# Weight sums and operand sums of the prologue formed by adding transfers, and the output weights copied later, in a hybrid Mamba-2 and attention layer

## Chip, cores and metric

The kernel runs on one core of one Trainium2 chip. The metric is the device time of one execution in microseconds (us), the median of several runs. Before the change it is 1277.86 us (three runs, 1277.46 to 1280.73).

## What is computed

One decoder layer on 1024 tokens of width 1024, all in float32. The change touches only the first product and the way its operands are made:

```python
h    = RMSNorm_pre(x)                                  # x, h: 1024 x 1024
proj = jnp.einsum('bld,de->ble', h, w_in)              # w_in: 1024 x 9248
z_ssm, xbc, dt_raw, q, k, v, f_raw, z_att, g_ssm, g_att = jnp.split(proj, ...)
...
merge = sigmoid(g_ssm) * (A @ w_branch_ssm) + sigmoid(g_att) * (B @ w_branch_att)
out   = merge @ w_out;  x <- x + RMSNorm_post(out)
```

A is a chunked SSD scan and B is causal attention with a forgetting bias; both follow later and are left alone.

## The kernel before

**Products.** The projections are done by a Strassen-Winograd scheme: seven products in place of eight. The right operand is h transposed, cut into four blocks of 512 x 512: B11, B21 (first 512 tokens), B12, B22 (last 512). Its seven forms are kept in SBUF as tiles x0 to x6: x0 = B11, x1 = B21, x2 = -B22, x3 = T1 = B12 - B11, x4 = -T2 with T2 = B22 - T1, x5 = T3 = T2 - B11, x6 = T4 = T2 - B21. Each has a high part and a low part (x5h and x5l), so that three fast matmuls stand for one float32 matmul. The high part is a ScalarE copy that rounds, the low part a VectorE subtraction (`put`, L1211).

**Weights.** The left operand comes in pairs of 128-column units (class `Pair`, L320). A pair has four blocks a11, a12, a21, a22 of 128 x 512, loaded into `raw` tiles (L342, six buffers). Product 1 takes a11, product 2 a12, product 4 a22, product 5 the sum s1 = a21 + a22, product 6 s2 = s1 + a11, product 3 s2 + a12, product 7 a11 + a21. The sums are VectorE additions (L355, L371). `split` (L345) then makes the high part on ScalarE (L349) and the low part on VectorE (L350) of a `wop` tile, of which there are four.

**Order.** `Stream` (L461) holds the list of (pair, product) steps. For the first three pairs p, q, r it begins p1, q1, p2, q2, p6, p5, p7, p4, p3, q6, q5, q7, r1, q4, q3. Each step is twelve matmuls at L128, done in two halves. `ahead` (L597) prepares the step three places later when a step starts, and `load_more` (L509) issues the next loads when the blocks that they replace have been used. TensorE's order is that of the program; a scheduler orders the other engines' instructions at build time.

**The prologue** (L1167 to L1280) loads eight token tiles `xt`, normalises them (the first four on VectorE, L1201, the last four on GpSimd, L1203), and transposes them on TensorE into `pt` (L1209). For the first 512 tokens ScalarE or VectorE scales the transposes into `low` (L1228, L1230), which holds B11 and B21. For the last 512 it goes through four columns j = 0 to 3. In each one, ScalarE scales two transposes into `up` (B12) and `b22` (both L1248), four float32 matmuls with 32 columns of weights go into `df` (L1251), VectorE forms t1 and t2, and half a product step follows. Then VectorE turns `low` into T3 and T4 in place (L1262, L1263). The tile t2 comes from a pool of four buffers named `th` that outputs use as well. After the columns come the parts of T3, T4 and -B22. `dft` (L1265) takes `df` out of PSUM.

**Queues.** All loads of weights and tokens are issued from SyncE's queue (SP), in order. Twelve copies of the output weights from the input to `wo_dram` (L1237, 256 KB each) stand there behind the first loads; they are read again near the end of the kernel. GpSimd's queue (POOL) issues transfers too, the first of them at 656.7 us of the span; no transfer adds to its destination.

Of the kernel before, what the change touches and what calls it, by code (L numbers as in the profile page):

```python
# [16 lines left out]
P = 128  # L17
T = 1024
D = 1024
NK = D // P  # L20
KH = NK // 2
# [65 lines left out]
def hybrid_layer(ctx: ExitStack, tc, a, out):  # L87

    nc = tc.nc
# [43 lines left out]
    def pin(op):  # L133
        return tc.keep_in_program_order(op)
# [185 lines left out]
    class Pair:  # L320
# [3 lines left out]


        USES = {"a11": (1, 6, 7), "a12": (2, 6), "a21": (6, 7), "a22": (6, 4)}

        def __init__(self, keys, handlers, ops=None, adds=nc.vector):
            self.keys, self.handlers = keys, handlers
            self.ops = xop if ops is None else ops  # L330
            self.adds = adds
            self.raw, self.op, self.prepared = {}, {}, set()
            self.s1, self.sums = None, 0

        def load(self, names):
            for n in names:
                if self.keys[0][0] == "merged":
                    h, t = int(n[2]) - 1, self.keys[int(n[1]) - 1][1]
                    self.raw[n] = fin["merged"][:, h * KH : (h + 1) * KH, t * P : (t + 1) * P]
                    continue  # L340
                t = wp.tile([P, KH, P], F32, tag="raw", bufs=6, name="raw")
                pin(nc.sync.dma_start(t, column_halves(self.keys[int(n[1]) - 1])[int(n[2]) - 1]))  # L342
                self.raw[n] = t

        def split(self, which, src):  # L345
            op = wp.tile([P, 2, KH, P], F32R, tag="wop", bufs=4, name="wop")
# [11 lines left out]
        def prepare(self, which):  # L358
            r = self.raw
            self.prepared.add(which)  # L360
            if which in (5, 6) and self.s1 is None:
# [99 lines left out]
    class Stream:  # L461
# [6 lines left out]
        def __init__(self, pairs, double, last):  # L468
# [40 lines left out]
        def load_more(self):  # L509

            while self.loads:
                old = self.loaded[-6:-4]
                if self.loads[0][0].keys[0][0] == "merged":
                    old = []
                    if "merged" not in fin:
                        return
                if not all(set(p.USES[n]) <= p.prepared for p, n in old):
                    return
                self.load_next()

# [646 lines left out]
    with tc.tile_pool(name="pro", bufs=1, reuse_waits="tile", side="right") as pro, tc.tile_pool(  # L1167
# [3 lines left out]
        nc.scalar.dma_start(wdf, a["wdf"])  # L1171
        preg = pro.tile([P, NK], F32, name="preg")
        nc.scalar.dma_start(preg, a["cst"][:, 80:88])
        ss = pro.tile([P, NT], F32, name="ss")
        rstd = pro.tile([P, NT], F32, name="rstd")
        low = pro.tile([P, NK, HALF], F32, name="low")
# [14 lines left out]
        def norm_tiles(hf, tiles):  # L1191
            for t, xt in enumerate(tiles, 4 * hf):
                sqt = small("sqt").bitcast(BF16)
                if t in (1, 3):
                    nc.vector.tensor_tensor_reduce(sqt, xt, xt, 1.0, 0.0, ALU.mult, ALU.add, ss[:, t : t + 1])
                else:
                    nc.scalar.activation(sqt, xt, AF.Square, accum_out=ss[:, t : t + 1])
                nc.scalar.activation(rstd[:, t : t + 1], ss[:, t : t + 1], AF.Sqrt, bias=epst, scale=1.0 / D)
                nc.vector.reciprocal(rstd[:, t : t + 1], rstd[:, t : t + 1])
                if hf == 0:  # L1200
                    nc.vector.tensor_scalar(xt, xt, rstd[:, t : t + 1], None, ALU.mult)  # L1201
                else:
                    nc.gpsimd.tensor_scalar(xt, xt, rstd[:, t : t + 1], None, ALU.mult)  # L1203

        def turned(tiles, k):
            pt = prop.tile([P, HALF], F32, tag="pt", bufs=2, name="pt")
# [16 lines left out]
        tiles2 = load_tiles(1)  # L1223
        stream.begin()
        for k in range(NK):
            pt = turned(tiles, k)
            if k > 1:
                nc.scalar.activation(low[:, k, :], pt, AF.Copy, scale=preg[:, k : k + 1])  # L1228
            else:
                nc.vector.tensor_scalar(low[:, k, :], pt, preg[:, k : k + 1], None, ALU.mult)  # L1230
            put("b11" if k < KH else "b21", k % KH, low[:, k, :])
            if k >= KH:
                stream.halves(1)
        norm_tiles(1, tiles2)

        for k, h in [(k, h) for j in range(KH) for k, h in ((j, 0), (j + KH, 0), (j + KH, 1))]:
            pin(nc.sync.dma_start(wo_dram[k, :, half(h)], a["wo"][k * P : (k + 1) * P, half(h)]))  # L1237

        b22 = []
        for j in range(KH):  # L1240
# [20 lines left out]
            with tc.issue_after(last[1]) if j == KH - 1 else nullcontext():  # L1261
# [3 lines left out]
        nc.scalar.activation(dft, df, AF.Identity, bias=bdf)  # L1265
        stream.halves(1)

        with tc.issue_after(last[0]), tc.issue_after(last[1]):
# [524 lines left out]
```

## Time and profile before

| | us |
|---|---|
| median of three runs | 1277.86 |
| profiled execution, its time | 1273.87 |
| profiled execution, its span | 1272.2 |
| TensorE busy in the span | 1246.1 |
| VectorE, ScalarE, GpSimd busy | 1012.9, 794.3, 319.3 |
| VectorE busy from 46 to 61 us | 15.0 of 15 |

The profile is one execution. Its views are the page (totals), the waits (who waited for whom), the chain of waits (the work that ended last, followed back step by step), the timeline (instructions in order, with start, duration and the idle time just before), and a table of busy time by stretches. In a timeline row "x3" joins three instructions. An L number is a line of the kernel before.

### The profile page before, as it was taken

To read this page: it belongs to the slowest core of one execution; us is meant where nothing else is said; L and a number is where in the kernel's file an instruction comes from. 1 tells how busy PE (TensorE), PEld (TensorE's weight loads), DVE (VectorE), ACT (ScalarE), POOL (GpSimd) and SP (SyncE) were. 2 spreads that over 40 slices of the span, in tenths; PEclk is the share of its full clock that TensorE was granted. 3 is DMA by queue.
4 is the path that set the end of the run, shared out by engine and by line. 5 is a ranking of instruction groups with operands and counts; after the bars stand their busy time and mean duration, and the time that the engine had idled before them with its cause. 6 is when DMAs were issued, how large, how long until landed. Compare 5 with 4: busy or idle time off the path is not lost.

```text
span 1272.2 us, 20822 instructions
## 1 busy us (share of the span) xinstructions
PE 1246.1 (98%) x6926; PEld 982.3 (77%) x6926; DVE 1012.9 (80%) x1994; ACT 794.3 (62%) x1737; POOL 319.3 (25%) x322
## 2 busy tenths in 40 slices
PE   5999999999999999999999999999999999999997
PEld 3678888888888888888887777777777777778886
DVE  7988886988888978997767676767789767886975
ACT  7745665556665765566555666666687666844753
POOL 4000440013400241115102124223112212356062
PEclk9999999999999999999999999999999999999999
DMA  8232452545436533744447576666687657766933
GB/s 300 69 120 76 146 162 88 191 152 182 138 101 215 175 127 117 219 146 140 142 149 252 162 228 212 217 214 218 232 286 263 224 184 249 249 221 199 364 110 105
DMA packets 152236, 233.56 MB, mean 184 GB/s; under 512 B 15201, under 2 KB 60737, under 8 KB 152129
## 3 DMA queue, kind: packets, MB, share of 16 engines
q1 hardware_dynamic: 136064, 196.08, 47.7%
q10 hardware_dynamic: 10560, 18.06, 3.8%
q0 software_dynamic: 5504, 18.09, 3.7%
q8 instruction: 54, 0.88, 0.3%
q14 instruction: 54, 0.43, 0.1%
HBM read 162.99 MB, written 72.34 MB: 185 GB/s over the span
## 4 chain that ended last, share of the span: by engine, by line
PE 86%; DMA 4%; DVE 4%; ACT 4%; issue 1%; SPq 0%; POOL 0%; DVEq 0%; ACTq 0%; POOLq 0%
PE pb L128 36%; PE pc L128 21%; PE pd L128 7%; PE av L128 5%; PE pt L131 5%; PE s L128 5%; PE yps L128 2%; PE st L128 1%; ACT ex L1509 1%; DMA xt<-in_x 1%; PE tr L131 1%; PE tr_v L131 1%; DMA v<-v_dram 1%; PE df L128 1%; DVE wop L350 1%
## 5 line engine op out<-in xcount | busy, mean ns | idle before, releaser
L350 DVE TENSOR_TENSOR wop<-sum,wop 128x512 fp32r<-128x512 f32 x180 | 140.2, 780 | 53.6 <-ACT wop L349 52.6
L349 ACT ACTIVATE wop<-sum 128x512 fp32r<-128x512 f32 x180 | 112.5, 626 | 109.0 <-DVE sum L355 52.4
L1509 ACT ACTIVATE ex<-ex,nm 128x512 f32<-128x512 f32 (+1 forms) x192 | 116.2, 606 | 71.9 <-DVE nm L1505 71.6
L402 ACT ACTIVATE s<-pb 128x512 f32<-128x512 f32 x144 | 85.3, 593 | 98.2 <-PE pb L128 96.2
L128 PE MATMUL pb<-x0h,wop 128*128 128x512 f32 x384 | 131.5, 399 | 0.0
L128 PE MATMUL pb<-x6h,wop 128*128 128x512 f32 x384 | 129.5, 395 | 1.3 <-ACT s L402 1.3
L128 PE MATMUL pb<-x5h,wop 128*128 128x512 f32 x384 | 130.1, 396 | 0.7 <-ACT s L402 0.7
L350 DVE TENSOR_TENSOR wop<-raw,wop 128x512 fp32r<-128x512 f32 x144 | 105.4, 733 | 31.8 <-ACT wop L349 31.5
L128 PE MATMUL pc<-x3h,wop 128*128 128x512 f32 x384 | 129.8, 396 | 0.5 <-DVE ot L419 0.4
L128 PE MATMUL pc<-x2h,wop 128*128 128x512 f32 x384 | 130.2, 397 | 0.0
L128 PE MATMUL pb<-x4h,wop 128*128 128x512 f32 x384 | 129.1, 395 | 0.0
L1505 DVE CUSTOM_DVE_ANT_0 ex<-s,fb 128x512 f32<-128x512 f32 (+1 forms) x192 | 96.8, 552 | 20.0 <-PE s L128 14.8
L349 ACT ACTIVATE wop<-raw 128x512 fp32r<-128x512 f32 x144 | 89.7, 623 | 14.7 <-PE pd L128 6.1
L128 PE MATMUL pd<-x1h,wop 128*128 128x512 f32 x288 | 96.3, 394 | 0.0
L128 PEld LDWEIGHTS pb<-x6h,wop 128*128 128x128 f32 x384 | 72.1, 188 | 18.6 <-issue 2.0
L128 PEld LDWEIGHTS pb<-x5h,wop 128*128 128x128 f32 x384 | 72.1, 188 | 18.4 <-issue 2.0
L128 PEld LDWEIGHTS pb<-x0h,wop 128*128 128x128 f32 x384 | 72.6, 189 | 17.6 <-issue 2.9
L128 PEld LDWEIGHTS pc<-x3h,wop 128*128 128x128 f32 x384 | 72.1, 188 | 17.7 <-issue 1.5
L128 PEld LDWEIGHTS pc<-x2h,wop 128*128 128x128 f32 x384 | 72.1, 188 | 17.4 <-issue 2.4
L128 PEld LDWEIGHTS pb<-x4h,wop 128*128 128x128 f32 x384 | 72.1, 188 | 16.7 <-issue 1.9
L211 POOL TENSOR_TENSOR wd<-wd 128x256 f32<-128x256 f32 x32 | 32.4, 1011 | 205.0 <-DMA wd<-in_wo 135.0
L131 PE MATMUL pt<-ident,ex 128*128 128x128 f32 x576 | 75.1, 273 | 2.0 <-ACT ex L1509 1.4
(318 smaller groups left out, 2993.6 us busy)
## 6 DMA issues: line engine op xcount, KB each, us to landing
raw<-in_wu SPq DMA_DIRECT2D x128, 256.0 KB
csb<-cs_dram SPq DMA_DIRECT2D x32, 256.0 KB
q<-q_dram SPq DMA_DIRECT2D x32, 256.0 KB
k<-k_dram SPq DMA_DIRECT2D x16, 512.0 KB
fb<-f_dram SPq DMA_DIRECT2D x16, 512.0 KB
rb<-st_dram SPq DMA_DIRECT2D x48, 128.0 KB
wd<-in_wo SPq DMA_DIRECT2D x40, 128.0 KB
xt<-in_x SPq DMA_DIRECT2D x8, 512.0 KB
```

The source lines that it names most:

```text
L128: return tc.keep_in_program_order(nc.tensor.matmul(*args, **kw))
L131: return tc.keep_in_program_order(nc.tensor.transpose(out_, in_, idn))
L211: pin(nc.gpsimd.tensor_tensor(t[out_], t[a_], t[b_], ALU.subtract))
L349: nc.scalar.activation(op[:, 0], src, AF.Copy)
L350: nc.vector.tensor_tensor(op[:, 1], src, op[:, 0], ALU.subtract)
L402: nc.scalar.activation(s, ps, AF.Copy)
L1505: nc.vector.tensor_tensor_reduce(o, s[e][:, 0:w], fb[hp, h][:, e, 0:w], 1.0, 3.0e38, ALU.add, ALU.min, nm)
L1509: pin(nc.scalar.activation(o, o, AF.Exp, scale=-1.0, bias=nm, accum_out=hd.at(hd.sm, i, h, e)))
```

## The change

For the first three pairs, `gather` starts s1 (and for p also s2) as a load of a21 from DRAM (issued from SP, L360 of the changed kernel) to which GpSimd's queue adds a22 and a11 by transfers with `accum_op` (L354 there). The sum a11 + a21 is made by adding a11 to the loaded a21 in place, and a12 is added to s2 after product 6 has taken it. q and r still form s2 with VectorE. That is eleven adding transfers. `low` is stored with its sign turned, so that T3 and T4 become sums: `low += t2` is an adding transfer from SBUF to SBUF for all of T4 and three quarters of T3; the last of T3 stays on VectorE. `behind` holds the first adding transfers until GpSimd has normalised its last token tile. `FEWER` says which products still read a loaded block. `ahead` prepares nothing when step 1 starts and two steps when step 2 starts. The twelve copies to `wo_dram` are issued behind the prologue.

```diff
+        FEWER = {"a11": (1, 6), "a12": (2,), "a21": (7,), "a22": (4,)}
...
+            if self.gathers and self.s1 is not None and "a21" in names:
+                self.add(self.raw["a21"], "a11")
+        def add(self, t, n):
+            with tc.issue_after(self.behind) if self.behind else nullcontext():
+                nc.gpsimd.dma_start(t, self.source(n), accum_op=ALU.add)
+        def gather(self):
+            for n in range(2 if self.gathers == "fully" else 1):
+                t = wp.tile([P, KH, P], F32, tag="sum", bufs=2, name="sum")
+                nc.sync.dma_start(t, self.source("a21"))
+                self.add(t, "a22")
+                if n == 0:
+                    self.s1 = t
+                else:
+                    self.add(t, "a11")
+                    self.s2 = t
+            if "a21" in self.raw:
+                self.add(self.raw["a21"], "a11")
...
             elif which == 6:
-                self.s2 = self.total(self.s1, r["a11"])
+                if self.gathers != "fully":
+                    self.s2 = self.total(self.s1, r["a11"])
                 self.split(6, self.s2)
+                if self.gathers:
+                    self.add(self.s2, "a12")
+                    return
...
+            elif which == 7 and self.gathers:
+                self.split(7, r["a21"])
...
+            p.gathers, q.gathers, r.gathers = "fully", "partly", "partly"
...
+            following = self.pairs[self.pairs.index(p) + 1 :][:1]
+            if which == 5 and following and following[0].gathers:
+                following[0].gather()
...
-            if self.at + 3 < len(self.steps):
-                p, which = self.steps[self.at + 3]
+            for n in {1: (), 2: (4, 5)}.get(self.at, (self.at + 3,)):
...
+        less = pro.tile([P, NK], F32, name="less")
+        nc.vector.tensor_scalar(less, preg, -1.0, None, ALU.mult)
...
-                nc.scalar.activation(low[:, k, :], pt, AF.Copy, scale=preg[:, k : k + 1])
+                nc.scalar.activation(low[:, k, :], pt, AF.Copy, scale=less[:, k : k + 1])
...
-        for k, h in [(k, h) for j in range(KH) for k, h in ((j, 0), (j + KH, 0), (j + KH, 1))]:
-            pin(nc.sync.dma_start(wo_dram[k, :, half(h)], a["wo"][k * P : (k + 1) * P, half(h)]))
+        stream.pairs[0].behind = stream.pairs[1].behind = norm_tiles(1, tiles2)
+        stream.pairs[0].gather()
...
-                nc.vector.tensor_tensor(t1, up[0], b11, ALU.subtract)
+                nc.vector.tensor_tensor(t1, up[0], b11, ALU.add)
...
-                nc.vector.tensor_tensor(b11, t2, b11, ALU.subtract)
-                nc.vector.tensor_tensor(b21, t2, b21, ALU.subtract)
+            if j < KH - 1:
+                nc.gpsimd.dma_start(b11, t2, accum_op=ALU.add)
+            else:
+                nc.vector.tensor_tensor(b11, t2, b11, ALU.add)
+            nc.gpsimd.dma_start(b21, t2, accum_op=ALU.add)
...
             put("-b22", j, b22[j], -1.0, order=pin)
+        for k, h in [(k, h) for j in range(KH) for k, h in ((j, 0), (j + KH, 0), (j + KH, 1))]:
+            pin(nc.sync.dma_start(wo_dram[k, :, half(h)], a["wo"][k * P : (k + 1) * P, half(h)]))
```

TensorE's instructions stand in the same order before and after, from the first to the last. On the other engines the order differs in the prologue and shortly behind it.

**ScalarE in the third column.** The first `up` and `b_419` below belong to the third column, `th` at L629 is the tanh of the first output of q, and its table load stands ahead of it. Before:

```order
L1213 ACTIVATE x4h<-th 128x512
L349 ACTIVATE wop<-sum 128x512
L1248 ACTIVATE up<-pt,preg 128x512
L1248 ACTIVATE b_419<-pt,preg 128x512
L629 ACT_TABLE_LOAD
L629 ACTIVATE th<-th 128x512
L630 DMA gs_dram<-th 128x512
L1213 ACTIVATE x3h<-th 128x512
L1248 ACTIVATE up<-pt,preg 128x512
```

After, with the names as above (`b_425` is the same tile, the three `wop` rows are s2, s1 and a11 + a21 of p):

```order
L1290 ACTIVATE up<-pt,preg 128x512
L666 ACT_TABLE_LOAD
L666 ACTIVATE th<-th 128x512
L1290 ACTIVATE b_425<-pt,preg 128x512
L667 DMA gs_dram<-th 128x512
L1257 ACTIVATE x3h<-th 128x512
L374 ACTIVATE wop<-sum 128x512 x2
L374 ACTIVATE wop<-raw 128x512
L1257 ACTIVATE x4h<-th 128x512
L1290 ACTIVATE up<-pt,preg 128x512
```

The table load and the tanh now stand between the third column's two copies out of PSUM, and three weight splits stand in front of the fourth column's.

**GpSimd's queue** from the last token tiles on. Before:

```order
L1203 TENSOR_SCALAR xt_182<-xt_182,rstd_144 128x1024
L1203 TENSOR_SCALAR xt_184<-xt_184,rstd_144 128x1024
L1203 TENSOR_SCALAR xt_186<-xt_186,rstd_144 128x1024
L1203 TENSOR_SCALAR xt_188<-xt_188,rstd_144 128x1024
L1291 AFFINE_SELECT tri_627<-onesr_625 128x128
```

After (`sum_330` is s1 of p, `sum_333` its s2, `raw_196` and `raw_368` the blocks a21 of p and q; `th_360` and `th_409` are t2 of the first two columns):

```order
L1246 TENSOR_SCALAR xt_194<-xt_194,rstd_150 128x1024
L354 DMA sum_330<-in_wu 128x512
L354 DMA sum_333<-in_wu 128x512
L354 DMA raw_196<-in_wu 128x512
L354 DMA raw_368<-in_wu 128x512
L1304 DMA low_151<-th_360 128x512
L1307 DMA low_151<-th_360 128x512
L354 DMA sum_333<-in_wu 128x512
L1304 DMA low_151<-th_409 128x512
L1307 DMA low_151<-th_409 128x512
```

Six adding transfers now stand in one queue ahead of the one that completes s2 of p.

**VectorE behind the fourth column**, from the first output of q's product 2 (`th<-pd,s`) on. Before:

```order
L415 TENSOR_TENSOR th<-pd,s 128x512
L1215 TENSOR_TENSOR x3l<-th,x3h 128x512
L350 TENSOR_TENSOR wop<-raw,wop 128x512
L1217 SCALAR_TENSOR_TENSOR x4l<-th,x4h 128x512
L1262 TENSOR_TENSOR low<-th,low 128x512
L1263 TENSOR_TENSOR low<-th,low 128x512
L1215 TENSOR_TENSOR x5l<-low,x5h 128x512 x3
L661 SCALAR_TENSOR_TENSOR th<-th 128x512
L1215 TENSOR_TENSOR x5l<-low,x5h 128x512
L1215 TENSOR_TENSOR x6l<-low,x6h 128x512 x3
L350 TENSOR_TENSOR wop<-sum,wop 128x512
```

After:

```order
L446 TENSOR_TENSOR th<-pd,s 128x512
L1261 SCALAR_TENSOR_TENSOR x4l<-th,x4h 128x512
L375 TENSOR_TENSOR wop<-raw,wop 128x512
L1259 TENSOR_TENSOR x5l<-low,x5h 128x512 x4
L698 SCALAR_TENSOR_TENSOR th<-th 128x512
L1259 TENSOR_TENSOR x6l<-low,x6h 128x512 x3
L375 TENSOR_TENSOR wop<-sum,wop 128x512
```

The two sums and an x3l have left this stretch. In both kernels it goes on with four x2l, the last x6l, a sum (s2 of q), `th<-pc,s`, a memset and `summing`, the tile that TensorE needs for the transpose of `dft`; after the change two more weight splits stand ahead of the memset. From `th<-pd,s` up to the memset there are 22 instructions of 128 x 512 before and 21 after.

More of the change, by code (lines that the diff above doesn't have):

```diff
@@ L333, in __init__ @@
             self.s1, self.sums = None, 0
+            self.gathers = self.behind = None
         def load(self, names):
@@ L360, in prepare @@
             self.prepared.add(which)
-            if which in (5, 6) and self.s1 is None:
+            if which in (5, 6) and self.s1 is None and not self.gathers:
                 self.s1 = self.total(r["a21"], r["a22"])
@@ L516, in load_more @@
                         return
-                if not all(set(p.USES[n]) <= p.prepared for p, n in old):
+                if not all(set((p.FEWER if p.gathers else p.USES)[n]) <= p.prepared for p, n in old):
                     return
@@ L597, in ahead @@
         def ahead(self, after):
[L599 to L600 removed]
+            for n in {1: (), 2: (4, 5)}.get(self.at, (self.at + 3,)):
+                if n >= len(self.steps):
+                    return
+                p, which = self.steps[n]
                 if after == (p.keys[0][0] == "merged"):
@@ L1173, in hybrid_layer @@
         nc.scalar.dma_start(preg, a["cst"][:, 80:88])
+        less = pro.tile([P, NK], F32, name="less")
+        nc.vector.tensor_scalar(less, preg, -1.0, None, ALU.mult)
+        sign = pro.tile([P, 1], F32, name="sign")
+        nc.vector.memset(sign, 1.0)
+        for n in (0, 2):
+            nc.vector.memset(sign[32 * n : 32 * n + 32, :], -1.0)
         ss = pro.tile([P, NT], F32, name="ss")
@@ L1202, in norm_tiles @@
                 else:
-                    nc.gpsimd.tensor_scalar(xt, xt, rstd[:, t : t + 1], None, ALU.mult)
+                    last = nc.gpsimd.tensor_scalar(xt, xt, rstd[:, t : t + 1], None, ALU.mult)
+            return last.ins if hf else None
         def turned(tiles, k):
@@ L1259, in hybrid_layer @@
             stream.halves(1)
-            with tc.issue_after(last[1]) if j == KH - 1 else nullcontext():
-                nc.vector.tensor_tensor(b11, t2, b11, ALU.subtract)
-                nc.vector.tensor_tensor(b21, t2, b21, ALU.subtract)
+            if j < KH - 1:
[3 more added lines that the diff above has]
+            nc.gpsimd.dma_start(b21, t2, accum_op=ALU.add)
         dft = small("dft")
-        nc.scalar.activation(dft, df, AF.Identity, bias=bdf)
+        nc.scalar.activation(dft, df, AF.Identity, bias=bdf, scale=sign)
         stream.halves(1)
```

7 lines of the change are left out of this document (4 added, 3 removed).

## Prediction, made before the changed kernel ran

> **What bounds the kernel now.** I read the page first, for how much of the span TensorE leaves idle at all.
>
> ```profile
> span 1272.2 us, 20822 instructions
> PE 1246.1 (98%) x6926; PEld 982.3 (77%) x6926; DVE 1012.9 (80%) x1994; ACT 794.3 (62%) x1737; POOL 319.3 (25%) x322
> ```
>
> Of 1272.2 us TensorE is idle for 26.1. Its instructions do not change, so a gain can only come out of these 26.1 us, or out of time in which a matmul counts as busy while it waits. The view of waits says, for TensorE in the first 75 us, where the change lies:
>
> ```profile
> PE pt L131 <- DVE rstd L1199: 8.6, 1, 8.6
> PE pt L131 <- DVE xt L1201: 2.8, 3, 1.5
> PE pt L131 <- ACT low L1228: 1.4, 1, 1.4
> PE pb L128 <- ACT s L402: 1.3, 1, 1.3
> PE pt L131 <- POOL xt L1203: 0.6, 1, 0.6
> PE pt_df L128 <- DVE summing L1304: 0.5, 1, 0.5
> PE pb L128 <- DVE x4l L1217: 0.3, 1, 0.3
> ```
>
> The first three, 12.8 us, come before any sum that goes. Within reach are the last four, 2.7 us. The table by stretches agrees: busy time of TensorE, its weight loads, VectorE, ScalarE and GpSimd, in the columns 27 to 46 us and behind the prologue.
>
> ```profile
> 27.00:46.00 19.00, 18.77 (x88) 9.88 (x89) 17.28 (x29) 13.41 (x22) 0.09 (x1) 1.00 0.13 44
> 61.00:90.00 29.00, 29.00 (x138) 23.65 (x137) 26.07 (x56) 14.41 (x27) 0.00 (x0) 1.00 0.42 145
> ```
>
> VectorE is nearly full in both, but TensorE is fuller, and from 61 us on it waits for nothing. Since that is so, only the moment at which TensorE comes out of the prologue counts. The chain of waits, asked for 8 to 62 us, shows who holds it until then (start, length, what):
>
> ```profile
> 24.11 0.52 ACT wop L349
> ...
> 27.83 0.52 ACT wop L349
> 28.34 0.58 ACT up L1248
> 28.97 1.62 PE df L128 x6
> ...
> 42.04 1.96 PE df L128 x8
> 44.00 1.59 PE pd L128 x6
> 45.62 0.69 DVE th L415
> ...
> 57.15 0.60 DVE sum L355
> 57.75 0.60 DVE x2l L1217
> ...
> 59.23 1.10 PE pt_df L128 x8
> ```
>
> Three links: ScalarE up to 28.9, TensorE's columns to 45.6, VectorE to 59.2. I go through them.
>
> **The sum.** All in microseconds against the profiled execution (1273.87).
>
> *Sign and `less`: +0.1.* VectorE gets one tiny multiply, `less`, in front of the token tiles that TensorE waits for.
>
> ```profile
> 9.28 0.16 DVE L1199 RECIPROCAL rstd<-rstd 128x1 f32<-128x1 f32 x1
> 13.27 0.75 DVE L1230 TENSOR_SCALAR low<-pt,preg 128x512 f32<-128x512 f32 x1 [0.57 <-PE pt L131]
> ```
>
> The nearest row takes 0.16. It needs `preg` at 9.4 us. All that the trace shows of that load is that at 13.27 it had landed, so the ends are 0 and 3.9. It is issued at the start and is small: I take 0.1.
>
> *First column, ScalarE's link: -0.7.* Two weight splits (24.11 and 27.83) leave ScalarE's queue ahead of the first `up`, 0.52 each. But `up` also needs the transposes of GpSimd's last tile:
>
> ```profile
> 27.14 0.76 PE L131 MATMUL pt<-ident,xt 128*128 128x128 f32 x5 [0.60 <-POOL xt L1203]
> 28.22 0.70 ACT L1248 ACTIVATE up<-pt,preg 128x512 f32<-128x512 f32 x1
> ```
>
> The transpose that waited for GpSimd at 27.14 is out at about 27.5, so `up` moves from 28.2 to 27.5 and `df` with it. The bounds are 0 (GpSimd as late or later) and -1.04 (both splits, if GpSimd is quicker with fewer VectorE sums beside it).
>
> *Third column: +1.9.* TensorE's last `df` matmul of a column needs ScalarE's second copy out of PSUM. Today:
>
> ```profile
> 37.23 0.67 ACT L1248 ACTIVATE up<-pt,preg 128x512 f32<-128x512 f32 x1
> 37.80 0.68 ACT L1248 ACTIVATE b<-pt,preg 128x512 f32<-128x512 f32 x1
> 38.50 1.28 ACT L629 ACT_TABLE_LOAD   x1
> 38.53 1.04 PE L128 MATMUL df<-b,wdf 128*32 128x512 f32 x2
> 39.79 0.63 ACT L629 ACTIVATE th<-th 128x512 f32<-128x512 f32 x1
> ```
>
> The copy starts 0.57 behind `up`, and `df` starts as it ends. In the new order table load and tanh stand between them: 0.67 for `up`, 1.29 from table load to tanh, and 0.53 to the next start make 2.5. TensorE has nothing else to do there, since its own order is fixed: +1.9. Nothing behind it gives this back, since TensorE carries the chain there. Bounds: 0, if TensorE were late for another reason; +2.0 if the tanh does not overlap the copy.
>
> [...]
>
> *The three splits ahead of the fourth column's `up`: 0.*
>
> ```profile
> 41.64 0.69 ACT L1248 ACTIVATE up<-pt,preg 128x512 f32<-128x512 f32 x1 [0.15 <-PE pt L131]
> ```
>
> This `up` waits for its transposes, and they come 0.1 - 0.7 + 1.9 = 1.3 later: 42.9. The third column's copy starts at 37.2 - 0.6 + 2.5 = 39.1, x3h at 39.6, the splits and x4h from 40.2 on at 0.52 each, to 42.3. TensorE hides them with 0.6 to spare. Uncovered, each would cost 0.52.
>
> *VectorE's link to `summing`: -0.6.* Its chain runs without a gap from 45.62 to 58.9 at 0.60 an instruction: 22 of them before, 21 after. The two sums and x3l that leave are three, the splits that move in are two. ScalarE's queue to the eviction `s`, the wait of 1.3, also gets one entry shorter (-0.5); the later of the two sets it, so their gains are not added. Bounds: 0 and -1.2, if the two splits make no difference.
>
> *The other VectorE sums taken away between 29 and 45 us: 0,* six of the low sums and two weight sums. TensorE is the link there; what gets shorter is VectorE's slack.
>
> *The copies to `wo_dram`: 0.*
>
> ```profile
> 12.00 10.54 SPq L1237 DMA_DIRECT2D wo_dram<-in_wo  x12
> 71.14 0.39 PE L128 MATMUL pb<-x0h,wop 128*128 128x512 f32 x1
> ```
>
> SP is held at q's `sum` load until p's s1 is split (about 42.3). Eleven copies at 0.88 then keep it until 52, and r's first weights come behind. Product r1 takes them at 71. Fifteen us and more cover the landing; what is late beyond that is paid one for one.
>
> *The adding transfers themselves: 0, if they land in time.* The trace has none. The nearest rows are plain 256 KB stores issued by GpSimd, here to `t_a`, and the rate from 10 to 20 us (last column, GB/s):
>
> ```profile
> L193 POOL DMA_DIRECT2D t_a<-y x7: 542/542/559, 756.0 to 1064.4; - x7
> DMA to landing us min/median/max: 2.3/4.8/7.3
> 10.00:20.00 10.00, 6.34 (x22) 4.77 (x23) 8.21 (x16) 8.80 (x19) 5.80 (x2) 1.00 1.04 401
> ```
>
> At 401 GB/s 256 KB take 0.65, which leaves 1.65 of the shortest landing for the rest. An adding transfer has to read its destination too, so I estimate T = 1.3 each on the engines, from twice 0.65; bounds are 0.65 and, from the longest landing (beside other traffic), 5.6, which taken seven times would cost 28 us. Where they are waited for:
>
> - s2 of p: GpSimd is free at 27.1, and its second adding transfer goes out at 27.6. The one that completes s2 is the seventh in the queue: 27.6 + 7T + 1.65, that is 38.4. ScalarE's split asks for it at 40.2 and holds up TensorE from 40.8. Behind that split stand x4h, `up` and `b` of the fourth column, so each us late is a us on TensorE. The point is T = 1.65.
> - Third column's `low` sums: issued behind t2 at 41; ScalarE's x5h asks for them three starts behind the end of the columns (45.6 + 1.3 = 46.9), at 48.4, and the next user of t2's buffer at 49.5: 7 us.
> - Fourth column's T4 sum and s1 of q, issued at 45 to 46.5 beside the copies: asked for by x6h, 16 starts of 0.52 behind 46.9, and by VectorE's sum, 14 of 0.60, both at 55.3: 9 us.
>
> Sum: 0.1 - 0.7 + 1.9 - 0.6 = **+0.7**, 1274.6 for an execution like the profiled one. That one lay 4.0 below the median, so for the median 1277.86 + 0.7 = **1278.6**. The adding transfers take some 5 us of work off VectorE, where it has slack.
>
> **The rivals.**
>
> *The adding transfers are late (slower).* With T = 2.5, s2 lands at 27.6 + 17.5 + 1.65 = 46.8, 6.0 past the 40.8 at which it starts to count: +6.7 in all, **1284.6**. For it: seven in one queue, and a destination that is read and written. Against it: from 27 to 46 us the transfer engines are 0.13 busy (the row above). It decides from T = 1.65, and passes 0.3% from about 2.1.
>
> [...]
>
> ```profile
> 19.19 1.05 PE L128 MATMUL pb<-x0h,wop 128*128 128x512 f32 x2
> 20.04 0.45 PE L128 MATMUL pb<-x0l,wop 128*128 128x512 f32 x1
> ...
> 21.46 0.63 PE L128 MATMUL pb<-x0h,wop 128*128 128x512 f32 x2
> 21.93 0.39 PE L128 MATMUL pb<-x0l,wop 128*128 128x512 f32 x1
> ```
>
> Two matmuls take 0.85 from start to start at 19.19, and 0.47 at 21.46. [...]
>
> *The gains come, the stall doesn't.* Were ScalarE's copy in time in spite of its new place, -1.2 would be left: **1276.7**. For it: only that a wait of TensorE inside a running `df` is not seen as idle today either. Against it: the 38.53 row follows the copy by 0.05.
>
> *VectorE sets the pace after all (faster).* If the columns follow VectorE, which is 17.28 of 19 busy, the nine sums that leave between 29 and 59 us are worth 0.60 each: -5.4 + 0.1, **1272.6**. Against it: TensorE waited for VectorE 0.8 us in that stretch.
>
> **Chances.** The forecast has 0.66, late transfers 0.22, no stall 0.07, VectorE 0.05. A difference of 0.3%, 3.8 us, is about what a measurement of this kernel can tell from no change. The forecast and the second rival lie within it, and of the first the 0.03 with T between 1.65 and 2.1: **same 0.76, slower 0.19, faster 0.05**. For the range I leave out VectorE's case and the worst of the late transfers: down to 1275.2, where the open terms all fall well (-1.04, -1.2, and the stall of +1.9 only half there: 1276.7) and the runs scatter by 1.5, half of what the three before span, and up to 1285.0, just past late transfers at T = 2.5.
>
> **What would show it.** In the changed profile: `df` waiting for ScalarE's `b` in the third column, some 1.5 to 2 us, with the table load right ahead; `up` of the first column at 27.5; the wait for `s` shorter by about half a us; no ScalarE or VectorE instruction waiting for a transfer between 40 and 57 us; TensorE full from 61 us on. The forecast is wrong if ScalarE's `wop<-sum` waits for a transfer, if `low` or `xt` comes later in the first 20 us (then `preg` was late), or if TensorE idles behind 61 us, where r's weights and sums arrive.

## The result and the profile after

The changed kernel takes 1280.49 us (median of 22 runs, 1276.47 to 1286.5), the kernel before in as many runs beside it 1277.41 (1274.72 to 1280.83). The ratio is 1.0025, 95% interval 1.0015 to 1.0036: the change costs 3.2 us (1.9 to 4.6). The sign of the difference is clear, though its size is within 0.3%. The median lies in the range of the prediction (1275.2 to 1285.0), whose upper part stood there for late transfers. The profiled execution took 1277.29; its page begins:

```profile
span 1275.6 us, 20870 instructions
PE 1247.5 (98%) x6926; PEld 982.4 (77%) x6926; DVE 1004.1 (79%) x1981; ACT 794.4 (62%) x1737; POOL 331.6 (26%) x340
```

VectorE has 8.8 us less to do (1012.9 before) and the span is 3.4 longer. The waits of TensorE in the first 75 us, by which engine and line it waited for (us, times, longest):

```profile
PE pt L131 <- DVE rstd L1242: 8.4, 1, 8.4
PE pt L131 <- DVE xt L1244: 2.9, 3, 1.6
PE pb L128 <- ACT s L433: 1.5, 1, 1.5
PE df L128 <- ACT b L1290: 1.5, 1, 1.5
PE pt L131 <- ACT low L1272: 1.3, 1, 1.3
PE pt_df L128 <- DVE u L802: 1.3, 1, 1.3
```

Two rows matter. `df` now waits for ScalarE's copy b, and `pt_df` waits 1.3 for VectorE where it was 0.5. The timeline of ScalarE and TensorE in the third column shows the first (the last row is TensorE's):

```profile
36.31 0.69 ACT L1290 ACTIVATE up<-pt,preg 128x512 f32<-128x512 f32 x1 [1.61 <-PE pt L131]
37.02 1.28 ACT L666 ACT_TABLE_LOAD   x1
38.31 0.63 ACT L666 ACTIVATE th<-th 128x512 f32<-128x512 f32 x1
38.84 0.67 ACT L1290 ACTIVATE b<-pt,preg 128x512 f32<-128x512 f32 x1
...
39.57 0.62 PE L128 MATMUL df<-b,wdf 128*32 128x512 f32 x1 [1.46 <-ACT b L1290]
```

From the second column's `df<-b` to the third's it is 6.42 us (33.15 to 39.57), before 4.50. The tanh in these rows belongs to p's first output; the section on the change calls it q's, which is wrong, since only p's product 2 has ended by then.

The chain of waits, asked for 24 to 62 us, shows who holds TensorE besides (start, length, what):

```profile
27.64 5.45 DMA sum<-in_wu
33.09 0.28 issue
33.37 7.94 DMA sum<-in_wu
41.31 0.02 issue
41.33 1.67 ACT wop L374 x3
43.01 0.52 ACT x4h L1257
43.52 0.58 ACT up L1290
44.11 0.04 issue
44.15 1.62 PE df L128 x6
...
48.65 8.21 DMA sum<-in_wu
...
61.53 0.55 PE pt_df L128 x3
```

Three adding transfers stand on it, where before there was none: the two that complete s2 of p, one behind the other, and s1 of q. Both sums are late for their readers (the last section of the experiments has a second profile, in which only s1 of q stands on the chain):

```profile
41.33 1.15 ACT L374 ACTIVATE wop<-sum 128x512 fp32r<-128x512 f32 x2 [1.30 <-DMA sum<-in_wu]
...
56.96 0.69 DVE L380 TENSOR_TENSOR sum<-sum,raw 128x512 f32<-128x512 f32 x1 [0.92 <-DMA sum<-in_wu]
```

And the transfer engines, 0.13 busy from 27 to 46 us before, are full (the two columns at the end: their busy share, GB/s):

```profile
27.00:46.00 19.00, 17.43 (x80) 8.42 (x81) 12.48 (x20) 13.16 (x22) 10.64 (x12) 1.00 0.96 168
61.00:90.00 29.00, 28.34 (x133) 23.21 (x134) 25.11 (x57) 14.45 (x29) 4.43 (x6) 1.00 0.65 191
```

A table of starts on TensorE, read from its timeline, is used for all kernels below. "b1, b3, b4" is `df<-b` of the first, third and fourth column, "p6" and "p4" the products of p behind them, "r1" the product from which TensorE was full before. The last column is the measured difference to the kernel before, worked out from the ratio at 1277 us, with its interval.

| kernel | b1 | b3 | b4 | p6 | p4 | pt_df | r1 | measured |
|---|---|---|---|---|---|---|---|---|
| before | 29.54 | 38.53 | 42.96 | 45.42 | 55.67 | 59.23 | 71.14 | |
| changed | 28.67 | 39.57 | 44.73 | 47.19 | 57.01 | 61.53 | 73.86 | 3.2 (1.9 to 4.6) |
| e1_tanh_behind | 29.36 | 38.35 | 44.53 | 46.99 | 56.83 | 61.78 | 75.00 | 4.5 (2.9 to 6.1) |
| e2_tanh_ahead_before | 29.85 | 40.80 | 45.74 | 48.20 | 58.45 | 62.90 | 74.72 | 2.7 (1.5 to 3.8) |
| e3_t34_vector | 29.72 | 41.69 | 46.11 | 48.59 | 61.33 | 64.19 | 76.00 | 6.4 (4.2 to 8.6) |
| e4_splits_late | 29.25 | 38.22 | 44.52 | 46.99 | 60.43 | 64.63 | 76.44 | 5.6 (4.1 to 7.2) |
| e5_plain | 29.08 | 38.05 | 43.74 | 46.21 | 56.02 | 59.55 | 71.47 | -0.4 (-1.9 to 1.1) |
| e6_copies_back | 29.33 | 40.24 | 44.74 | 47.21 | 58.33 | 62.79 | 74.60 | 3.2 (1.4 to 5.0) |
| e7_only_t34 | 29.91 | 40.83 | 45.25 | 47.72 | 57.53 | 61.38 | 73.30 | 2.7 (1.0 to 4.2) |
| e8_split_behind | 29.05 | 38.57 | 43.25 | 45.72 | 55.97 | 59.73 | 71.63 | 0.9 (-0.5 to 2.4) |
| e9_plain_as_is | 29.35 | 40.26 | 44.68 | 47.16 | 56.98 | 60.49 | 72.41 | 0.8 (-0.5 to 2.0) |
| e10_few_adds | 28.98 | 37.97 | 42.65 | 45.12 | 56.46 | 60.58 | 72.50 | 0.6 (-0.8 to 2.2) |

The delay of r1 against 71.14 follows the measured time in every row within 1.6 us: most of what these kernels gain or lose lies in the prologue. The delay is that of one profile each, the measured time that of 6 to 22 runs.

In the profiles of `e2`, `e3`, `e4` and `e6` something more stands in it. TensorE runs at about half its pace for a few us of the prologue, behind a wait of 1.83, 1.24, 3.07 and 2.80 us, and its mean granted clock from 46 to 61 us reads 0.89 in `e3`, 0.96 in `e4` and 0.94 in `e6`, where the changed kernel's reads 1.00. In `e2` that looks so:

```profile
58.45 0.50 PE L128 MATMUL pb<-x6h,wop 128*128 128x512 f32 x1 [1.83 <-ACT s L402]
58.79 0.58 PE L128 MATMUL pb<-x6l,wop 128*128 128x512 f32 x1
59.17 1.06 PE L128 MATMUL pb<-x6h,wop 128*128 128x512 f32 x2
```

Two matmuls take 0.85 from start to start there (59.17 to 60.02), and 0.46 in p5 of the same profile: about half the pace. `e3` (56.41 to 57.26) and `e4` (61.45 to 62.30) have the same 0.85, `e6` 0.86 (59.99 to 60.85). The product behind the wait (p4; in `e3` p3) takes 1.3 to 1.6 us more than at the full pace: p4 with its way to pt_df 4.45 in `e2`, 4.20 in `e4`, 4.46 in `e6`, but 2.86 in `e3`. At half the pace such a loss takes twice its length, so an estimated 2.7 to 3.2 us are run that way. The rows of the other profiles, the changed kernel's among them, show no such pace from 27 to 83 us.

### The profile page after: what moved, and what is told of

It reads as the page before. It is cut to its first block, busy times and chain, and to the rows that moved or that the text cites. A ratio compares the mean times of both kernels' runs of the same rounds, so it can differ in the third digit from the quotient of the medians.

```text
span 1275.6 us, 20870 instructions
## 1 busy us (share of the span) xinstructions
PE 1247.5 (98%) x6926; PEld 982.4 (77%) x6926; DVE 1004.1 (79%) x1981; ACT 794.4 (62%) x1737; POOL 331.6 (26%) x340
## 4 chain that ended last, share of the span: by engine, by line
PE 82%; DMA 6%; DVE 5%; ACT 4%; issue 2%; POOL 1%; SPq 0%; DVEq 0%; ACTq 0%; POOLq 0%
PE pb L128 35%; PE pc L128 21%; PE pd L128 7%; PE av L128 5%; PE s L128 4%; PE pt L131 4%; PE yps L128 2%; DMA sum<-in_wu 2%; ACT ex L1555 1%; PE st L128 1%; DMA xt<-in_x 1%; DVE wop L375 1%; PE tr L131 1%; PE tr_v L131 1%; DMA st_dram<-st 1%
## 5 line engine op out<-in xcount | busy, mean ns | idle before, releaser
L375 DVE TENSOR_TENSOR wop<-sum,wop 128x512 fp32r<-128x512 f32 x177 | 136.9, 776 | 55.3 <-ACT wop L374 54.0
```

What stands on the lines that cost most here:

```text
L375: nc.vector.tensor_tensor(op[:, 1], src, op[:, 0], ALU.subtract)
```

## The experiments

**Theory A**, after the result: there are two delays that lie over each other, the table load ahead of b in the third column, and adding transfers that land too late. **Rival B**: the table load is all of it. **C**: the transfers for T3 and T4 are what delays the others. **D**: it is the place on GpSimd's queue, the order of the engines or the traffic, and not the adding. **E**: the copies to `wo_dram`, now beside them, delay s1 of q.

### The table load put behind the copy, and the other way round

In `e1_tanh_behind` the work behind p's first output is kept back until the third column's copies are issued.

```diff
+        gate, delayed = first.handlers, []
+        first.handlers = ((gate[0][0], delayed.append) + tuple(gate[0][2:]),) + tuple(gate[1:])
...
-                nc.scalar.activation(up[-1], pt, AF.Copy, scale=preg[:, k : k + 1])
+                copied = nc.scalar.activation(up[-1], pt, AF.Copy, scale=preg[:, k : k + 1])
+            if j == 2:
+                with tc.issue_after(copied.ins):
+                    for ch in delayed:
+                        gate[0][1](ch)
```

> The changed kernel with p's tanh and its table load held back behind the third column's copy b. Theory A (two delays that lie over each other: the table load, 1.9, and the adding transfer that completes s2 of p, landing at 41.3): the third column's df no longer waits, so it starts near 37.7 instead of 39.6, but s2 still lands at about 41.3, its split still holds up the fourth column's up at about 43.5, and TensorE waits there instead, some 2.6 us. Time as the changed kernel, within 0.5 us, so 3 us above the kernel before. Rival B (the table load is the loss): 1.9 us faster than the changed kernel, 1.2 above the kernel before.

The third column's stall is gone (b3 comes 8.99 behind b1, as before), and the fourth column's has grown: b4 comes 6.18 behind b3, before 4.43. At r1 nothing is left of the gain. B falls. What A had too simple is that s2 is not alone in the queue: its split waited only 0.4 for the transfer, and the splits themselves, with x4h, now hold up `up`. p6 starts 0.1 to 0.2 earlier than in the changed kernel; the rest of the loss comes behind it, where VectorE's sum waits 1.35 for s1 of q.

`e2_tanh_ahead_before` is the kernel before with the copy held behind the tanh instead (`tanhs` keeps the tanh's instruction).

```diff
+                with tc.issue_after(tanhs[0]) if k == KH + 2 else nullcontext():
```

> The kernel before with only this: the third column's copy b stands behind the table load and the tanh, as in the changed kernel. Theories A and B alike: b starts at about 39.8 instead of 37.8, df with it, nothing behind gives it back: 1.9 us slower than the kernel before (bounds 1.2 and 2.1). If the stall were cover for another wait (VectorE's chain, the eviction s), 0 to 0.5.

Measured 2.7 us. Its third column is 1.95 late (b2, at 34.35, to b3: 6.45), as the sum had it, and the fourth 0.5 more, because there x4h slipped between the two copies. So the table load's place alone, without a single adding transfer, costs nearly what the whole change costs. Up to 1.6 of the 3.58 at r1 are the stretch at half the pace, though, and how many of its runs had one is not recorded.

### Adding against plain transfers

`e5_plain` is `e1_tanh_behind` without the adding, so that its sums are left out; all five engines have the same rows in the same order.

```diff
-                nc.gpsimd.dma_start(t, self.source(n), accum_op=ALU.add)
+                nc.gpsimd.dma_start(t, self.source(n))
...
-                nc.gpsimd.dma_start(b11, t2, accum_op=ALU.add)
+                nc.gpsimd.dma_start(b11, t2)
...
-            nc.gpsimd.dma_start(b21, t2, accum_op=ALU.add)
+            nc.gpsimd.dma_start(b21, t2)
```

> The kernel of e1_tanh_behind with plain transfers in place of the adding ones: same queue, same places, same bytes, but nothing is added, so the sums for the first weights, T3 and T4 are left out. Theory A (what is lost is that the adding transfers land late, because each takes the engines 1.5 us and not 0.7): the landing times fall from 6 to 10 us to 3 to 5, s2 and s1 of q are there when asked for, and 0.8 us above to 0.8 below the kernel before. What is left of a stall is ScalarE's three splits in front of the fourth column's up, some 1.2. Rival D (issuing on GpSimd's queue, or the order of the engines, costs it): 3 us or more above the kernel before, as e1_tanh_behind.

It measures -0.4 us, 4.9 less than `e1_tanh_behind`. The view of transfers from 26 to 62 us gives the queue (packets, MB, share of 16 engines) and the issues (KB each, median us to landing). The changed kernel, then `e5_plain`:

```profile
q0 software_dynamic: 2016, 3.67, 60.5%
...
low<-th POOLq DMA_DIRECT2D x7, 256.0 KB, 8.1
sum<-in_wu POOLq DMA_DIRECT2D x6, 256.0 KB, 6.8
```

```profile
q0 software_dynamic: 1184, 3.93, 30.6%
...
low<-th POOLq DMA_DIRECT2D x7, 256.0 KB, 4.2
sum<-in_wu POOLq DMA_DIRECT2D x6, 256.0 KB, 3.7
```

3.67 MB are 14 transfers of 256 KB and 60.5% of 36 us is 21.8: an adding transfer takes all engines 1.56 us. For the plain one it is 11.0 us by 15, 0.73. D falls as to place and order: the same issues in the same places cost nothing once they don't add. The load on the transfer engines halves with it, so this run can't part the adding from the traffic that it makes.

`e9_plain_as_is` does the same to the changed kernel as it is.

> The changed kernel as it is, its table load ahead of the third column's copy b included, with plain transfers in place of the adding ones, so that the sums are left out as in e5_plain. This is the fourth corner: place of the table load by adding or plain. Theory A: the third column's stall stays (df<-b at 1.9 behind the second column's pace), s2 and s1 of q are in time, 1.5 to 2.7 us above the kernel before, and the two prices lie over each other: the changed kernel is no slower than either price alone by more than 1 us. If the prices simply added, the changed kernel (3.1 above) would have to lie 4.9 above this one, as e1_tanh_behind does above e5_plain; then this one would be faster than the kernel before.

Measured 0.8 (-0.5 to 2.0), where A had expected 1.5 to 2.7. The changed kernel is 2.4 above it, by the two intervals some 0.6 to 4.2, where A had allowed 1; by r1 of three profiles it is 1.3 to 1.9. Its stalls on TensorE from 20 to 100 us:

```profile
PE pb L128 <- ACT s L433: 1.5, 1, 1.5
PE df L128 <- ACT b L1290: 1.5, 1, 1.5
PE pt_df L128 <- DVE u L802: 0.5, 1, 0.5
```

The four corners are then: plain and tanh behind -0.4, plain and tanh ahead 0.8, adding and tanh behind 4.5, adding and tanh ahead (the change) 3.2. The table load costs 1.2 where nothing is late, and nothing where the adding transfers are. The times alone don't settle the first of these (each corner is known to 1.2 to 1.6); at r1 it is 0.9.

The table also says where the adding costs it. p6 starts at 47.16 in `e9_plain_as_is` and at 47.06 to 47.19 in three profiles of the changed kernel: up to there adding costs nothing. From p6 to pt_df it is 13.33 against 14.34 to 14.66, where VectorE waits for s1 of q, and from pt_df to r1 11.92 against 12.17 to 12.58.

### Which transfers are late

`e3_t34_vector` puts the sums for T3 and T4 back on VectorE:

```diff
-            if j < KH - 1:
-                nc.gpsimd.dma_start(b11, t2, accum_op=ALU.add)
-            else:
-                nc.vector.tensor_tensor(b11, t2, b11, ALU.add)
-            nc.gpsimd.dma_start(b21, t2, accum_op=ALU.add)
+            with tc.issue_after(last[1]) if j == KH - 1 else nullcontext():
+                nc.vector.tensor_tensor(b11, t2, b11, ALU.add)
+                nc.vector.tensor_tensor(b21, t2, b21, ALU.add)
```

> The changed kernel with all eight sums for T3 and T4 back on VectorE; the weight sums stay transfers. The scheduler then puts p's three splits ahead of the third column's up, at about 36.4. Theory A: s2's second adding transfer is issued at 33.1 and, with fewer others beside it, lands 5.5 to 8 us later, 38.6 to 41; the third column's up waits for it 3.9 to 6.3 us, while s1 of q is in time: 0 to 2.5 us slower than the changed kernel, 3 to 5.5 above the kernel before. Rival C (the transfers for T3 and T4 are what delays the others): s2 and s1 are in time and 1.8 us come back, 1.2 above the kernel before.

```profile
38.82 1.15 ACT L374 ACTIVATE wop<-sum 128x512 fp32r<-128x512 f32 x2 [3.06 <-DMA sum<-in_wu]
```

s2 lands at 38.8, 2.5 us sooner, but its split stands one column earlier and holds that column up by the 3.06. Measured 6.4: C falls, and the loss is above A's 3 to 5.5; 1.6 of it, in the profile, is p3 at half the pace (4.34 us, in `e4` 2.75 at the full pace). The chain of waits goes on over a plain transfer, the tanh's output, which took 5.97 us (43.61 to 49.58); behind it t2 of the fourth column waits for the buffer.

`e4_splits_late` was meant to beat both kernels: the tanh behind the copy as in e1, the splits of p behind the fourth column's copies, the sums of q and r on VectorE.

```diff
-            p.gathers, q.gathers, r.gathers = "fully", "partly", "partly"
+            p.gathers = "fully"
...
-            for n in {1: (), 2: (4, 5)}.get(self.at, (self.at + 3,)):
+            for n in {1: (), 2: (), 3: ()}.get(self.at, (self.at + 3,)):
...
+            if j == KH - 1:
+                with tc.issue_after(copied.ins):
+                    for which in (6, 5, 7):
+                        stream.prepare(first, which)
```

> The changed kernel with the tanh behind the third column's copy, p's three splits behind the fourth column's two copies, and the weight sums of q and r back on VectorE. Transfers are left for p's sums and for T3 and T4. Theory A: no stall is left in the columns, they end at 44.75 (45.62 before, less the 0.87 of the first up); pt_df follows 13.0 to 13.6 us later; 0.9 to 1.5 us faster than the kernel before. Rival D (the adding transfers cost by their traffic or by their place on GpSimd's queue, whoever waits for them): still 1 us or more above the kernel before.

It is 5.6 slower. Here A, as stated, fell: s2 was no longer waited for, and three other adding transfers were; 1.3 more is p4 at half the pace. Its chain:

```profile
31.25 9.79 DMA low<-th
41.04 0.03 issue
...
41.16 0.70 DVE th L1308
...
47.96 9.20 DMA sum<-in_wu
57.16 0.02 issue
57.19 0.26 ACT wop L374
```

The third column's t1 waited 3.46 us for the first column's transfer into `low` to let go of t2's buffer (in the changed kernel the second column's t1, at 32.55, reads the same `low` with transfers into it under way and does not wait, so it is the buffer). T4's last x6h waited 0.42, and the split for product 3 waited 2.03 for a12. **Theory A'**: not one late sum, but every adding transfer takes some 4 to 10 us here, and any of them with less room than that, for its result or for the buffer that it reads, is paid for. Which one pays depends on the order around it.

`e10_few_adds` follows from A': only p's adding transfers stay, with 10 us of room each. It is `e4_splits_late` with the sums for T3 and T4 on VectorE by the diff of e3.

> The changed kernel with only the five adding transfers of p left (s1, s2, a11 + a21, and later a12 to s2); T3, T4 and the weight sums of q and r on VectorE, the tanh behind the third column's copy, p's three splits behind the fourth column's copies, so that every adding transfer has 10 us or more from issue to its reader. Theory A: no instruction waits for an adding transfer, no stall is left in the columns, which end 0.9 us earlier than before; VectorE's chain behind them has one instruction more (23 for 22), +0.6: 0.3 us faster than the kernel before, within 0.6. Rival D (adding transfers cost by their traffic, whoever waits): 1.5 us or more above.

Measured 0.6 (-0.8 to 2.2). No instruction but GpSimd's own issue waits for a transfer of a sum, and the columns end at 45.12, earlier than before. Behind them TensorE loses more than that to VectorE, and r1 comes 1.36 later than before (waits of TensorE, 20 to 100 us):

```profile
PE pb L128 <- DVE x4l L1261: 2.0, 1, 2.0
PE pb L128 <- ACT s L433: 0.7, 1, 0.7
```

A's 0.3 faster was not reached, and D's 1.5 is not excluded by the time alone; but no engine that TensorE depends on waits for an adding transfer. With room they cost nothing that shows there, and gain nothing.

`e7_only_t34` keeps those for T3 and T4 and forms all weight sums on VectorE.

```diff
-            p.gathers, q.gathers, r.gathers = "fully", "partly", "partly"
...
-        stream.pairs[0].behind = stream.pairs[1].behind = norm_tiles(1, tiles2)
-        stream.pairs[0].gather()
+        norm_tiles(1, tiles2)
```

> The changed kernel with all weight sums back on VectorE; T3, T4, the sign and the copies stay as changed. The scheduler still puts the table load ahead of the third column's copy b, and p's splits are back ahead of the first up. Theory A: the adding transfers for T3 and T4 alone land in time for their readers, so only the table load's place is left, which cost 2.7 in e2_tanh_ahead_before, less up to 0.6 of VectorE's chain: 2 to 3 us above the kernel before. Rival C (the transfers for T3 and T4 are themselves late, by the buffer of t2 that they hold): 4 us or more above.

Measured 2.7, as A had it. VectorE's t1 did wait 3.5 us in two places for transfers into `low`, but the columns, already held by the table load's place, lost nothing to it: b4 comes 4.42 behind b3.

### The copies, and the early `up`

`e6_copies_back` moves the twelve copies back to their old place.

```diff
+        for k, h in [(k, h) for j in range(KH) for k, h in ((j, 0), (j + KH, 0), (j + KH, 1))]:
+            pin(nc.sync.dma_start(wo_dram[k, :, half(h)], a["wo"][k * P : (k + 1) * P, half(h)]))
         stream.pairs[0].gather()
```

> The changed kernel with the twelve copies to wo_dram back at their old place in SyncE's queue, ahead of the loads for the sums. Theory A: s1 of q is late because its load waits for p's split and its adding transfer for the load, and because adding transfers are slow even alone; without the copies beside it, it lands in 6 to 8 us and not 8.2: 0 to 1.1 us faster than the changed kernel, 2 to 3 above the kernel before. Rival E (the copies, put beside the adding transfers, make them late): s1 is in time, and 1.4 us or more come back.

Measured 3.2, so nothing comes back, but E is half right: without the copies beside it VectorE no longer waits for s1 of q (issued at 49.19, read at 56.96), and the sums' transfers from 26 to 62 us land in a median of 5.6 us, in the changed kernel 6.8. The edit did more than move the copies, since the scheduler now puts s1 of q ahead of the sum for T4's last quarter; how much of the difference is due to that is not shown. That sum is late in its place, because s1 of q stands ahead of it in GpSimd's queue and was issued only behind a wait of 5.10 us (GpSimd, and ScalarE's reader):

```profile
49.19 0.87 POOL L354 DMA_DIRECT2D sum<-in_wu  x1 [5.10 <-DVE x4l L1261]
49.72 1.23 POOL L1309 DMA_DIRECT2D low<-th  x1
...
55.08 0.63 ACT L1257 ACTIVATE x6h<-low 128x512 fp32r<-128x512 f32 x1 [1.19 <-DMA low<-th]
```

`e8_split_behind` takes over the one gain into the kernel before.

```diff
-                    self.prepare(p, which)
+                    with tc.issue_after(self.behind) if self.at == 2 else nullcontext():
+                        self.prepare(p, which)
...
+            stream.behind = copied.ins
```

> The kernel before with one thing taken over from the change: the second split of p's weight sums no longer stands ahead of the first column's up on ScalarE, but behind that column's copies. Nothing else of the change. Theory A: up starts 0.5 to 0.9 earlier, TensorE's columns follow it, and 0.5 to 0.9 us are gained if VectorE's chain does not take them back. Rival (VectorE's chain to summing sets the end of the prologue by itself): no change.

b1 comes 0.5 earlier, and 0.5 is back by the third column:

```profile
36.22 0.63 ACT L349 ACTIVATE wop<-sum 128x512 fp32r<-128x512 f32 x1 [2.74 <-PE pd L128]
36.75 0.61 ACT L1214 ACTIVATE x3h<-th 128x512 fp32r<-128x512 f32 x1
37.27 0.67 ACT L1249 ACTIVATE up<-pt,preg 128x512 f32<-128x512 f32 x1
```

The split waits for the end of p's product 2, and x3h and `up` stand behind it. 0.9 (-0.5 to 2.4): no gain, and no version here beats the kernel before.

### The changed kernel again

Its runs spread over 10.0 us, those of the kernel before over 6.1; two more profiles were taken to see where.

> The changed kernel itself, a second profile. Its 22 runs spread over 10.0 us, those of the kernel before over 6.1, and the first profiled execution was one of its fastest (1277.3). Theory A: the landing times of the adding transfers are what spreads; in a slower execution s2 of p lands later than at 41.3, or s1 of q later than at 56.9, and TensorE's r1 starts later than at 73.9 by as much. Rival: the prologue's events stay within 0.5 us of the first profile, and the spread comes from behind 75 us.

> The same once more, a third profile: as for e11_changed_again.

They took 1276.63 and 1277.97, and p6 starts at 47.07 and 47.06, r1 at 73.71 and 74.30. From the second to the third `df<-b` it is 6.42 and 6.43. The prologue repeats within 0.6 us, so these profiles don't support A on the spread.

They do correct the first profile in one thing. In `e11_changed_again` b1 starts 0.6 later (29.27), and s2 of p is hardly late (a row of its waits, 27 to 70 us):

```profile
ACT wop L374 <- DMA sum<-in_wu: 0.4, 1, 0.4
```

b4 comes 4.43 behind b3, as before the change, and s2 is not on the chain of waits; s1 of q still is, and VectorE waits 1.05 for it. So s2 holds TensorE up only in an execution whose columns start early, and s1 of q in all three.

None of the three is of an execution above 1278. The longer ones go with the granted clock, of which the record has a mean for each run: the six of the 22 at 0.995 or 0.996 took 1281.32 to 1286.5, the seven at 0.999 or 1.000 took 1276.47 to 1281.78. The kernel before, in 81 runs beside the experiments, never reads below 0.997. So part of the 3.2 us may be stretches at half the pace behind longer waits, as in `e2`, `e3`, `e4` and `e6`; where in the long runs they lie, and whether the late transfers bring them on, no profile here shows.

## Why the prediction was right and wrong

The forecast of 1278.6 was 0.7 above the median; measured are 3.2. That the time still lies near the forecast is no merit of its mechanism, which had the transfers in time. Step by step:

- **Sign and `less`, +0.1:** right within 0.2. TensorE's waits for `rstd` and `xt` are 8.4 and 2.9, before 8.6 and 2.8.
- **First column, -0.7:** right in its place, but 0.87, 0.27 and 0.50 in three profiles, and not kept where it is large. e8 shows that this work comes back on ScalarE two columns later. In the changed kernel p6 starts at 47.06 to 47.19 in three profiles with b1 between 28.67 and 29.27: with b1 early the landing of s2 sets it, with b1 at 29.27 the columns do.
- **Third column, +1.9:** right to 0.02 (6.42 less 4.50), and e2 shows that it alone does that. "Nothing behind it gives this back" held in e9, whose p6 is 1.74 later than before. But the place of the load alone is worth less, because something else is uncovered without it: at p6 0.95 with plain transfers (e9 less e5, the splits) and 0.1 to 0.2 with adding ones (the change less e1). The load itself took 1.28 us in both kernels, with 0.02 ahead of it and 0.01 behind it in the changed one.
- **Three splits, 0:** right for plain transfers (e9: b4 4.42 behind b3, before 4.43), and only because the third column is late; without that (e5) they cost 1.3 of the 5.69 from b3 to b4.
- **VectorE's link, -0.6:** right in e9 (p6 to pt_df 13.33, before 13.81: -0.5). In the changed kernel it is 14.34, +0.5, by the wait for s1 of q. The wait for `s`, which was to be half a us shorter, is 1.5 in both (before 1.3), though the stretch from p6 to p4 that ends with it is 0.43 shorter in both.
- **Copies, 0:** right for what was named, the landing of r's weights: no stall stands there in e9. That they share the engines with s1 of q was left out: it lands in 8.2 us beside them, and without them it is read 7.8 after its issue with no wait (e6). The whole still came to 3.2 with the copies back, but in another order of GpSimd's queue; the same order was not tried.
- **The adding transfers, "0, if they land in time":** the step that failed. T was estimated at 1.3, below its point of 1.65; it measures 1.56, still below, and the transfers are late all the same. So the point itself was wrong. "27.6 + 7T + 1.65" takes the queue as the only limit, but the one that completes s2 can be issued only when the one before it has landed: 27.64, 5.45 to land, 0.28, 7.94 more, 41.31, where the formula with 1.56 gives 40.2. And s1 of q, given 9 us from an issue at 45 to 46.5, was issued at 48.65, since its load is issued at 43.32 behind p's split and has to land first, and then took 8.21. Together they cost 2.4 (the changed kernel less e9; 0.6 to 4.2), and by the profiles s1 of q is the one that costs it.

So e9, the kernel that the forecast describes, measured +0.8 for a sum of +0.7 (known to about 1.3, and +1.27 at r1); the change measured what the first rival describes, late transfers, at 2.4 and not at its 6.0. The tell named for that rival, ScalarE's `wop<-sum` waiting for a transfer, stands in the profile.

A slower TensorE behind a wait has no term in the sum: four other kernels here paid 1.3 to 1.6 us for it behind waits of 1.2 to 3.1 us. The profiles of the changed kernel show none from 27 to 83 us.

## What to carry to other kernels

Moving a sum from an engine with slack to a transfer was here a trade of 0.6 us of work for 4 to 10 us of latency: find for each one the latest issue and the earliest reader, chained ones added up, and count the buffers that it keeps as readers too. An engine's order can change where the diff does not look (here a table load went ahead of a copy), and that cost 2.7 us by itself in the kernel before. Two delays on one path did not add: undoing the table load's place alone showed no gain here, undoing the adding alone did. And read the granted clock of each stretch before a loss is put down to the wait in front of it.

## What the runs showed of the hardware

- An adding transfer of 256 KB takes the transfer engines 1.56 us, a plain one from the same queue 0.73: 2.1 times. It goes as 144 packets (2016 by 14), the plain one as 79. That a second reading, of the destination, makes the factor was the prediction's estimate; no run here parts reading from writing.
- The transfer engines were full at 168 GB/s, as the profile counts bytes: 0.96 busy with adding transfers (the row of 27 to 46 us), where in the kernel before they moved 401 GB/s at 1.04 (10 to 20 us).
- GpSimd's issue of an adding transfer shows as 0.85 to 1.9 us, of a plain one mostly 0.54 (e5), but two adding ones in a row start 0.53 apart as well (49.19 and 49.72 above). There the first had waited 5.10 us, and the one behind it in the queue was issued only then.
- TensorE ran at about half its pace (0.85 from start to start of two matmuls, else 0.46) for an estimated 2.7 to 3.2 us behind waits of 1.2 to 3.1 us in four profiles (e2, e3, e4, e6), at a price of 1.3 to 1.6 us each; its granted clock from 46 to 61 us was 0.89 in e3, 0.96 in e4 and 0.94 in e6. It did not in the changed kernel behind waits of 1.3 to 1.5, nor in e10 behind one of 2.0, so here the length of a wait alone does not decide it.
